# A gated MLP's down-projection by one level of Strassen instead of plain tiles, with sums of weights and gated values kept in DRAM

## The chip, the cores and the metric

One core of one Trainium2 chip. The time is device microseconds of one execution; the kernel before takes 2624.11 us (median of 3 runs, 2624.06 to 2625.13). The engines are named as in the profile: PE (TensorE, matmuls), PEld (its weight loads), DVE (VectorE), ACT (ScalarE), POOL (GpSimd), SP (SyncE, which issues every DMA).

## The reference, cut to what matters

Two layers of an encoder over 1024 tokens of 1024 channels, float32. Each layer has a token mixer (layer 0 attention, layer 1 pooling), a cross-attention into 256 memory tokens, and a gated MLP; residual adds around each. The part that changes is the end of the MLP:

```python
def conv_gated_ffn(h, w_up, conv_w, conv_b, w_down):
    u = h @ w_up                                   # 1024 x 1024 by 1024 x 5632
    up = jnp.pad(u, ((0, 0), (1, 1), (0, 0)))
    u = up[:, :-2] * conv_w[0] + up[:, 1:-1] * conv_w[1] + up[:, 2:] * conv_w[2] + conv_b
    gate, val = u[..., :D_FF], u[..., D_FF:]
    return (jax.nn.silu(gate) * val) @ w_down      # 1024 x 2816 by 2816 x 1024
```

## The kernel before

**Precision.** Every large product is made in three matmuls (`mm3`, L583 to L588): each operand is split into a high part (ACT, L498) and the rest (DVE, L501), and high x high, high x low and low x high are added up in PSUM. An operand of 512 columns thus costs one ACT and one DVE instruction of 512 before PE can use it.

**Buffers.** `scr` is a pool of six tiles of 128 x 1024 that serves every load and scratch value. `R` holds 20 slots, or 40 "halves" of 128 x 1024, for split operands. `X0` to `X7` are the residual rows, 128 tokens each. PSUM has two tiles of two banks (`pA`) and four of one bank (`pB`) in this part.

**Order of the MLP**, the same in both layers:

1. *Output projection of the cross-attention*, `Seven.begin`, 16 steps written out by hand. Step (n, t) makes columns n of token tile t with 24 matmuls, and DVE adds them to `X[t]` (L1087). Where n is 1 the row is complete: SP stores it to `Xd` in DRAM (L231), ACT, POOL and DVE normalise it in place (L567, L559, L236), and PE transposes it one step later (`turn`, L241; steps 3, 4, 6, 8, 10, 12 and 15). The transposed tiles go on as operands of a Strassen form of seven products (`Seven`). `extras` hangs loads and sums of the first weight blocks on some steps.
2. *Up-projection*: 22 blocks f of 128 gate and 128 value channels, each in seven products of 12 matmuls (`Seven.product`). For each block SP loads two tiles of weights (L292), DVE makes four sums of them (L311), ACT and DVE split seven operands, and read the products from PSUM (L355, L357). Then come the convolution (L1110, L1115, L1120), SiLU (L1127) and the gate (L1131); the gated block, 128 channels x 1024 tokens, is stored to `G` in DRAM (L1134). The eight `X` tiles serve as weight buffers here, four to a block.
3. *Down-projection*: six rounds of up to four blocks. A round loads its blocks of `G` and of `w_down` into `scr` (L1154), splits them into halves, and for each token tile t and column half n adds 3 matmuls per block in one bank, which DVE adds to `X[t]` (L1239). The rows come back from `Xd` (L1224). Rounds are prefetched while the round before runs; the last one, blocks 20 and 21, is interleaved with what follows: in layer 0 the pooling mixer (its weights are loaded by `late`, called one round earlier; its first matmul is L1315), in layer 1 the final norm.

**Who sets the order.** In step 2 and the first loads of step 3 a planner (`Plan`) is given every instruction with a price, dependencies, buffer needs and a due time; it lists them greedily and the program is emitted in that order, so each engine's queue is fixed by it. A load is priced as 0.40 us of SP and 4.2 us until it has landed, whatever else is in flight. PE's own order is fixed by hand (`order`). In steps 1 and 3 the order is that of the code.

Of the kernel before, what the change touches and what calls it, by code (L numbers as in the profile page):

```python
# [16 lines left out]
P = 128  # L17
# [24 lines left out]
N_SLOTS = 20  # L42

# [73 lines left out]
class Plan:  # L117
# [4 lines left out]
    KINDS = {"product": ("PE", 2.72, 2.92), "turn": ("PE", 0.87, 1.07), "add": ("DVE", 0.60, 0.72),  # L122
             "add2": ("DVE", 1.14, 1.25), "tap": ("DVE", 1.20, 1.31), "copy": ("ACT", 0.51, 0.65),
             "copy2": ("ACT", 0.96, 1.10), "centre": ("ACT", 1.15, 1.28), "silu": ("ACT", 0.96, 1.10),
             "load": ("SP", 0.40, 4.20), "store": ("SP", 0.40, 4.20)}
# [8 lines left out]
    def add(self, kind, emit, reads=(), writes=(), take=(), uses=(), gives=None, late=None):  # L134


        engine, busy, lag = self.KINDS[kind]
# [22 lines left out]
    def run(self):  # L160
# [6 lines left out]
        left = {e: [op for op in self.ops if op["engine"] == e] for e in self.free}  # L167
        uses = {k: len(ops) for k, ops in self.users.items()}
        takers = [op for op in self.ops if op["take"]]

        def begin(op):

            if any(o["end"] is None for o in op["after"]):
                return None
            t = max([self.free[op["engine"]], op["begin"]] + [o["end"] for o in op["after"]])
            need = {}
            for pool, _ in op["take"]:
                need[pool] = need.get(pool, 0) + 1
            for pool, n in need.items():
                first = sum(p == pool for o in takers if o["end"] is None and o["due"] < op["due"] for p, _ in o["take"])  # L180
                if len(self.room[pool]) < n + first:
                    return None
                t = max(t, sorted(self.room[pool])[n - 1])
            return t if op["engine"] == "PE" else max(t, op["due"] - self.AHEAD)

        while any(left.values()):
            best = None
            for e, ops in left.items():
                found = [(t, op) for op in (ops[:1] if e == "PE" else ops) if (t := begin(op)) is not None]
# [27 lines left out]
class Seven:  # L217
# [76 lines left out]
    def first_load(self, f, n):  # L294

        self.raws[f] = [self.kn.scr() for _ in range(n)]
        self.place[f] = [f"raw{f}{j}" for j in range(4)]
        for j in range(min(n, 2)):
            self.load(f, j)

    AT = {"A11": (0, 0), "A12": (0, 1), "A21": (1, 0), "A22": (1, 1), "S1": (2, 0), "S2": (2, 1), "S3": (3, 0), "S4": (3, 1)}
    SUMS = {"S1": ("A21", "A22", OP.add), "S2": ("S1", "A11", OP.subtract), "S4": ("A12", "S2", OP.subtract),
            "S3": ("A11", "A21", OP.subtract)}
# [61 lines left out]
    def begin(self, gemm, add, free, between):  # L365
# [5 lines left out]
        extras = {1: between, 2: lambda: self.first_load(0, 4), 6: lambda: self.first_load(1, 1),  # L371
                  7: lambda: [self.sum(0, n) for n in self.SUMS],
                  14: lambda: (split(0, "A12", "A11"), late("T2", 1), late("T2", 3)),
                  15: lambda: late("T3", 1)}
        for i, (n, t) in enumerate(steps):
# [7 lines left out]
            if n:  # L383
                self.rows(t)
            if u is not None:
# [6 lines left out]
    def plan_rest(self, plan):  # L392
# [4 lines left out]
        def keep(name, t, src, *keys, uses=()):  # L397
            parts = lambda: self.parts(name, t)
            shaped = lambda: src().rearrange("p (a b) -> p a b", a=4)
            plan.add("copy", lambda: self.kn.high(list(parts())[0], shaped()), keys, [("H", name, t)], uses=uses)  # L400
            plan.add("add", lambda: self.kn.low(*parts(), shaped()), [*keys, ("H", name, t)], [("H", name, t)], uses=uses)

        def sub(out, p, q, reads, writes, uses=(), late=None):
            plan.add("add", lambda: self.sub(nc.vector, out(), p(), q()), reads, writes, uses=uses, late=late)
# [7 lines left out]
        plan.add("turn", lambda: self.turn(t), [X(t, 0), X(t, 1)], banks, [("B", k) for k in banks])  # L412
        plan.add("copy", lambda: nc.scalar.copy(y[:, lo], self.ps[t][0]), banks[:1], [X(t, 0)], uses=banks[:1])
# [15 lines left out]
    def plan_load(self, plan, f, *js):  # L429
        for j in js:  # L430
            plan.add("load", partial(self.load, f, j), (), [(self.place[f][j], h) for h in range(2)], uses=[self.place[f][j]])
# [5 lines left out]
    def plan_left(self, plan, f, sums, names):  # L437
        for n in sums:
            spots = [self.spot(f, m) for m in (*self.SUMS[n][:2], n)]
            plan.add("add", partial(self.sum, f, n), spots[:2], spots[2:], uses={s[0] for s in spots})  # L440
        for n in names:
            at, op = self.spot(f, n), ("op", f, n)
            plan.add("copy", partial(self.high, f, n), [at], [op], [("half", op)], at[:1])
            plan.add("add", partial(self.low, f, n), [at, op], [op], uses=[at[0], op])

    def plan_product(self, plan, f, n, last):
# [7 lines left out]
        plan.add("product", emit, [op] + [("H", right, t) for t in (1, 3, 5, 7)], [(bank, f)],  # L454
# [4 lines left out]
        plan.add(how, partial(self.read, f, n, how),  # L459
# [4 lines left out]
class Kernel:  # L464
# [634 lines left out]
    def ffn_main(self, i, U, X, Xd, late, begin):  # L1099
        nc, R = self.nc, self.R  # L1100
        wd = self.a["ffn_w_down"][i]
        G = self.tc.dram_tile([FF, S], F32, name=f"G{i}")
        C = {}

        def taps(name, j):

            def centre(f):
                u, c = U.bank[f][name], self.scr()
# [16 lines left out]

        def silu(f):
# [6 lines left out]
        def store(f):  # L1133
            nc.sync.dma_start(out=G[f * P:(f + 1) * P, :], in_=C.pop(("v", f)))  # L1134

        def plan_conv(plan, name, f):
            u, c = (name, f), ("conv", name, f)
            ins = [(u, 0), (u, 1)]
            centre, left, right = taps[name]
            plan.add("centre", partial(centre, f), ins, [c], [("scr", c)], [u])  # L1140
            plan.add("tap", partial(left, f), [*ins, c], [c], uses=[u, c])
            plan.add("tap", partial(right, f), [*ins, c], [c], uses=[u, c])

        def plan_gated(plan, f, late):
            g, v = ("conv", "g", f), ("conv", "v", f)
            plan.add("add2", partial(gated, f), [g, v], [v], uses=[g, v])
            plan.add("store", partial(store, f), [v], uses=[v], late=late)

        rounds = [list(range(f, min(f + 4, NF))) for f in range(0, NF, 4)]
        hl, raw = {}, {}  # L1150

        def fetch(kind, f):
            raw[kind, f] = self.scr()
            nc.sync.dma_start(out=raw[kind, f], in_=(G if kind == "g" else wd)[f * P:(f + 1) * P, :])  # L1154

        def high(kind, f):
            hs = hl[kind, f] = [R.get_half(), R.get_half()]
            self.high(R.hv(hs[0]), raw[kind, f])

        def low(kind, f):  # L1160
            self.low(*(R.hv(h) for h in hl[kind, f]), raw.pop((kind, f)))

        def operand(kind, f):

            fetch(kind, f)
            high(kind, f)
            low(kind, f)

        def plan_operand(plan, kind, f, late):
            o, parts = ("raw", kind, f), [("part", kind, f, j) for j in range(2)]  # L1170
            plan.add("load", partial(fetch, kind, f), (), [o], [("scr", o)])
            plan.add("copy2", partial(high, kind, f), [o], parts, [("half", None)] * 2, [o])
            plan.add("add2", partial(low, kind, f), [o, *parts], parts, uses=[o], late=late)

        def up():
            begin()
            names = ("A12", "A11", "S1", "S2", "S4", "S3", "A22")
            U.H["T4"] = [R.get(), R.get()]
            plan = Plan({"DVE": 6.5, "ACT": 4.9}, {"scr": 2, "A": 2, "B": 4, "half": len(R.freed)})
            for f, js in ((0, (1, 2, 3)), (1, (0,))):  # L1180
                for j in js:
                    plan.hold("scr", U.place[f][j])
            for name in names[:2]:
                plan.hold("half", ("op", 0, name))
            places = {1: (1, 3, 5), 0: (7, 0, 2, 4), 2: (6, 1, 3, 5)}
# [8 lines left out]
            U.plan_left(plan, 0, (), names[2:])  # L1194
            done = set()
            for item in order:
                if item is None:
                    U.plan_rest(plan)
                    U.plan_load(plan, 1, 1)
                    U.plan_left(plan, 1, U.SUMS, names)  # L1200
# [252 lines left out]
```

## Time and profile before

| what | us |
|---|---|
| median of the runs shown | 2624.11 |
| the profiled execution | 2624.52 |
| its span, first to last instruction | 2622.6 |
| output projection with `begin`, layer 0 | 847 to 946 |
| up-projection, layer 0 | 946 to 1363 |
| down-projection without its last two blocks, layer 0, from the count of its matmuls | 1363 to 1581 |
| the same three in layer 1 | 1858 to 1956, 1956 to 2373, 2373 to 2592 |
| mean granted clock of PE | 0.995 |

The profile is of one execution. Times count from the first instruction. In lists of instructions the columns are start, duration, engine, source line, operation, and the shapes of what is written and read; the bracket gives the engine's idle time just before and what ended it. In tables by stretch they are the stretch, its length, busy time and count of PE, PEld, DVE, ACT and POOL, the clock, the share of the 16 DMA engines that was busy, and GB/s.

### The profile page before, as it was taken

The page shows a single profiled execution, that of the slowest core. Times are in us where ns is not written, and L with a number is a line of the kernel's source. Part 1 is how long each engine was busy: PE and PEld are TensorE (multiplying, and loading weights), DVE is VectorE, ACT ScalarE, POOL GpSimd, SP SyncE. Part 2 cuts the span into 40 slices and gives each one's busy share as a digit, 9 for nine tenths or more (in the row PEclk, how much of TensorE's full clock was granted, in tenths as well). Part 3 has the DMA queues.
Part 4 walks back from the last instruction along what each step waited for, and adds up shares of the span by engine and source line. Part 5 has one row for each costly group of instructions (what it writes and reads, how often), then busy time and mean ns, then how long its engine had stood idle before and what let it go on. Part 6 is the DMA issues. An engine that isn't in the chain of part 4 may idle for free. (4 is left out here: it accounts for less than half of the span.)

```text
span 2622.6 us, 35895 instructions
## 1 busy us (share of the span) xinstructions
PE 2573.9 (98%) x13817; PEld 2203.1 (84%) x13817; DVE 1732.5 (66%) x2479; ACT 1222.9 (47%) x2048; POOL 376.2 (14%) x521
## 2 busy tenths in 40 slices
PE   8989999999999999999999999999999999999998
PEld 7988888888898888888888888889888888888886
DVE  6778999964346379777775435534569777777334
ACT  4448888852245255555552104425446555454111
POOL 3664445520011000000000001102000000000001
PEclk9999999999999999999999999999999999999999
DMA  4200000031223123323254203321313232327201
GB/s 154 85 6 1 1 1 1 1 137 49 88 65 106 49 70 93 95 73 97 73 185 185 96 25 89 106 65 50 106 49 105 78 92 73 97 97 272 90 24 64
DMA packets 167552, 209.20 MB, mean 80 GB/s; under 512 B 6741, under 2 KB 134077, under 8 KB 167381
## 3 DMA queue, kind: packets, MB, share of 16 engines
q1 hardware_dynamic: 167381, 206.91, 24.4%
q8 instruction: 108, 1.77, 0.3%
q14 instruction: 63, 0.52, 0.1%
HBM read 166.42 MB, written 35.65 MB: 77 GB/s over the span
## 5 line engine op out<-in xcount | busy, mean ns | idle before, releaser
L586 PE MATMUL pB<-R,R 128*128 128x512 f32 (+1 forms) x2864 | 1071.2, 375 | 3.8 <-ACT R L506 1.9
L587 PE MATMUL pB<-R,R 128*128 128x512 f32 (+1 forms) x2848 | 1061.3, 373 | 1.7 <-DVE R L507 1.4
L588 PE MATMUL pB<-R,R 128*128 128x512 f32 (+1 forms) x2784 | 1035.7, 372 | 0.0
L586 PEld LDWEIGHTS pB<-R,R 128*128 128x128 f32 x2864 | 538.7, 188 | 101.5 <-ACT R L506 3.1
L587 PEld LDWEIGHTS pB<-R,R 128*128 128x128 f32 x2848 | 536.4, 188 | 96.0 <-DVE R L507 4.0
L588 PEld LDWEIGHTS pB<-R,R 128*128 128x128 f32 x2784 | 524.1, 188 | 92.0 <-DVE R L507 0.2
L1239 DVE TENSOR_TENSOR X<-pB,X 128x512 f32<-128x512 f32 x192 | 131.2, 688 | 225.0 <-PE pB L588 224.9
L501 DVE TENSOR_TENSOR R<-X,R 128x512 fp32r<-128x512 f32 x310 | 209.9, 686 | 91.2 <-ACT R L498 91.2
L559 POOL TENSOR_SCALAR ms<-ss 128x1 f32<-128x1 f32 (+2 forms) x102 | 26.6, 260 | 1697.4 <-ACT scr L567 781.2
L498 ACT ACTIVATE R<-X 128x512 fp32r<-128x512 f32 x310 | 193.3, 631 | 89.9 <-PE pB L587 71.8
L498 ACT ACTIVATE R<-scr 128x1024 fp32r<-128x1024 f32 (+1 forms) x106 | 100.3, 981 | 246.3 <-PE pB L587 160.7
L580 PE MATMUL pB<-ident,scr 128*128 128x128 f32 x1376 | 182.3, 276 | 10.8 <-DVE scr L572 9.1
L580 PEld LDWEIGHTS pB<-ident,scr 128*128 128x128 f32 x1376 | 157.3, 142 | 37.8 <-POOL scr L672 14.7
L672 POOL TENSOR_SCALAR scr<-scr,inv 128x1024 f32<-128x1024 f32 x128 | 144.0, 1125 | 167.1 <-DVE inv L671 162.2
L507 DVE TENSOR_TENSOR PT<-pB,PT 128x512 fp32r<-128x512 f32 x256 | 163.9, 680 | 3.2 <-ACT PT L506 2.3
L669 ACT ACTIVATE scr<-pA,nm 128x1024 f32<-128x1024 f32 x128 | 142.9, 1116 | 44.7 <-DVE nm L666 41.5
L355 ACT COPY scr<-pB 128x512 f32<-128x512 f32 x132 | 77.4, 586 | 183.5 <-PE pB L588 182.2
L666 DVE TENSOR_REDUCE nm<-pA 128x1 f32<-128x1024 f32 x128 | 156.1, 1220 | 0.9 <-PE pA L662 0.4
L506 ACT ACTIVATE R<-pB 128x512 fp32r<-128x512 f32 (+1 forms) x182 | 94.4, 551 | 127.4 <-PE pB L588 80.4
L507 DVE TENSOR_TENSOR R<-pB,R 128x512 fp32r<-128x512 f32 (+1 forms) x182 | 108.6, 627 | 65.1 <-ACT R L506 64.8
L662 PE MATMUL pA<-R,R 128*128 128x512 f32 x512 | 146.6, 408 | 0.0
L506 ACT ACTIVATE PT<-pB 128x512 fp32r<-128x512 f32 x256 | 138.7, 596 | 13.1 <-PE pB L580 10.9
(127 smaller groups left out, 3495.9 us busy)
## 6 DMA issues: line engine op xcount, KB each, us to landing
X<-in_ffn_w_up SPq DMA_DIRECT2D x82, 512.0 KB
G<-scr SPq DMA_DIRECT2D x44, 512.0 KB
scr<-in_ffn_w_down SPq DMA_DIRECT2D x44, 512.0 KB
scr<-G SPq DMA_DIRECT2D x44, 512.0 KB
scr<-in_xattn_w_kv SPq DMA_DIRECT2D x32, 512.0 KB
scr<-in_attn_w_qkv SPq DMA_DIRECT2D x20, 512.0 KB
scr<-in_xattn_w_q SPq DMA_DIRECT2D x16, 512.0 KB
scr<-in_xattn_w_o SPq DMA_DIRECT2D x16, 512.0 KB
```

What stands on the lines that cost most here:

```text
L498: self.nc.scalar.activation(hi, src, AF.Copy)
L501: self.nc.vector.tensor_tensor(out=lo, in0=src, in1=hi.bitcast(F32), op=OP.subtract)
L506: nc.scalar.activation(hi, src, AF.Copy)
L507: nc.vector.tensor_tensor(out=lo, in0=src, in1=hi.bitcast(F32), op=OP.subtract)
L580: self.nc.tensor.transpose(p[:, k, :], src[:, b * P:(b + 1) * P], self.ident)
L586: mm(out, ah, bh, start=start, stop=False)
L587: mm(out, ah, bl, start=False, stop=False)
L588: mm(out, al, bh, start=False, stop=stop)
L662: nc.tensor.matmul(s[:, kh * 512:(kh + 1) * 512], q, R.v(K[part][kh], 4)[:, kv], start=part == 0, stop=part == 1)
L666: nc.vector.tensor_reduce(nm, s, axis=AX.X, op=OP.max, negate=True)
L669: nc.scalar.activation(pr, s, AF.Exp, bias=nm, accum_out=rs)
L672: nc.gpsimd.tensor_scalar(pr, pr, ri, 1.0, op0=OP.mult, op1=OP.mult)
```

## The change

The 20 first channel blocks are taken in ten pairs. A pair's values are a matrix of 1024 tokens x 256 channels, its weights one of 256 x 1024; both are cut in two each way, and the pair's part of the result is made in seven products of half the size instead of eight (the same form that the up-projection uses, with the values on the left). The products go in three rounds of 3, 4 and 3 pairs. Blocks 20 and 21 stay as they were, as the last part.

- *Weights*: four differences of each pair's weights are made on DVE during the output projection and stored in DRAM (`ahead`), to be loaded again in the rounds with the four plain quarters that are needed (`plan_W`).
- *Values*: an even block's gated values now stay in `X4`; when the odd block is done, DVE makes four sums, two into `X6` and two in place (`plan_sums`), and SP stores seven pieces of 512 columns to DRAM (`G7`), 256 KB each, instead of two blocks. A round loads them again piece by piece (`plan_G`).
- *Products*: for a round, half of the tokens (g), a product n and a token tile pair (j) there are 3 matmuls per pair into one bank; each of the seven products is read by DVE into `X` (`plan_down`). All of it is given to the planner with the up-projection.
- *Up-projection*: a block has three weight buffers instead of four (S3 and S4 overwrite sources), since `X4` and `X6` are taken; its first loads come at steps 11 and 12 of `begin` instead of 2 and 6, three of block 0's sums at step 13 instead of four at 7.
- *Planner*: an instruction's price is a constant and a part per column; it gives 0.60 us for a DVE instruction of 512 and 2.72 for 12 matmuls, as the fixed prices did.
- `late` (pool weights, layer 0) is called after the plan, just before the last part.

```diff
+NQ = NF // 2 - 1
+ROUNDS = ((0, 1, 2), (3, 4, 5, 6), (7, 8, 9))
...
-    AT = {"A11": (0, 0), "A12": (0, 1), "A21": (1, 0), "A22": (1, 1), "S1": (2, 0), "S2": (2, 1), "S3": (3, 0), "S4": (3, 1)}
+    AT = {"A11": (0, 0), "A12": (0, 1), "A21": (1, 0), "A22": (1, 1), "S1": (2, 0), "S2": (2, 1), "S3": (1, 0), "S4": (2, 1)}
...
-        extras = {1: between, 2: lambda: self.first_load(0, 4), 6: lambda: self.first_load(1, 1),
-                  7: lambda: [self.sum(0, n) for n in self.SUMS],
+        extras = {1: between, 11: lambda: self.first_load(0, 3), 12: lambda: self.first_load(1, 1),
+                  13: lambda: [self.sum(0, n) for n in ("S1", "S2", "S3")],
...
             if n:
                 self.rows(t)
+            ahead(i)
             if u is not None:
                 self.take1(u)
...
-        def store(f):
-            nc.sync.dma_start(out=G[f * P:(f + 1) * P, :], in_=C.pop(("v", f)))
...
+        def plan_sums(plan, q, v, late):
...
+            add(S1, of(one, 1), of(other, 1), OP.add, [o, v], [("X6", 0)], [v])
+            add(S2, S1, of(one, 0), OP.subtract, [("X6", 0), e], [("X6", 1)])
+            add(of(one, 1), of(one, 0), of(one, 1), OP.subtract, [e, o], [o])
+            add(of(one, 0), of(other, 0), S2, OP.subtract, [v, ("X6", 1)], [e], [v])
...
+                plan.add("load", 1, lambda n=n, src=src: keep(n, src(), q), [k], [("G", q, n)], uses=[k], late=late + 2.0)
...
+        def plan_G(plan, r, qs, g, n):
...
+            plan.add("load", 1, fetch, [("G", q, n) for q in qs], [raw], [("scr", raw)])
+            plan.add("copy", w, high, [raw], parts, [("half", k) for k in parts], [raw])
+            plan.add("add", w, low, [raw, *parts], parts, uses=[raw, *parts])
...
+        def ahead(i):
+
+            if i < NQ:
+                raws[i] = [self.scr() for _ in range(2)]
+                for j in range(2):
+                    nc.sync.dma_start(out=raws[i][j], in_=wd[(2 * i + j) * P:(2 * i + j + 1) * P, :])
+            if 0 < i <= NQ:
+                (b11, b12), (b21, b22) = ((r[:, :512], r[:, 512:]) for r in raws.pop(i - 1))
+                for n, (out, p, q) in {"T1": (b11, b12, b11), "T3": (b12, b22, b12), "T2": (b22, b22, b11),
+                                       "T4": (b21, b21, b22)}.items():
+                    nc.vector.tensor_tensor(out=out, in0=p, in1=q, op=OP.subtract)
+                    nc.sync.dma_start(out=WT[i - 1][int(n[1]) - 1], in_=out)
+
+        WAT = (("B21", "B22"), ("B11",), ("T1", "T2"), ("T3", "T4"))
+
+        def plan_W(plan, q, late):
...
+            for j, names in enumerate(WAT):
+                raw = ("wraw", q, j)
+                plan.add("load", 1, partial(fetch, j), (), [raw], [("scr", raw)])
+                for h, n in enumerate(names):
+                    k = ("w", q, n)
+                    plan.add("copy", 512, partial(high, n, j, h), [raw], [k], [("half", k)], [raw])
+                    plan.add("add", 512, partial(low, n, j, h), [raw, k], [k], uses=[raw, k], late=late)
...
+        def plan_down(plan, r, qs, g, j, n):
...
+                for k, q in enumerate(qs):
+                    wh, wl = U.halves(WD[q, right])
+                    self.mm3(banks[b], hi[:, k], lo[:, k], wh, wl, fresh and k == 0, k == len(qs) - 1, not fresh)
...
+            def read():
+                x = X[t][:, h * 512:(h + 1) * 512]
+                nc.vector.tensor_tensor(out=x, in0=banks[b], in1=x, op=OP.add)
+            plan.add("product", 3 * len(qs), emit, parts + ws, [b], [("A" if bank == "x" else "B", b)] if fresh else (),
+                     parts + ws + ([] if fresh else [b]))
+            plan.add("add", 512, read, [b, ("row", t, h)], [("row", t, h)], uses=[b], late=1.5)
+
+        def plan_phase(plan, homes):
...
+            for r, qs in enumerate(ROUNDS):
+                for k, q in enumerate(qs):
+                    plan_W(plan, q, -3.0 * (len(qs) - 1 - k) if k < len(qs) - 1 else None)
+                for g in range(2):
+                    for n in (2, 1, 5, 6, 3, 7, 4):
+                        plan_G(plan, r, qs, g, U.PRODUCTS[n][0])
+                    for n in (2, 1, 5, 6, 3, 7, 4):
+                        for j in range(2):
+                            plan_down(plan, r, qs, g, j, n)
+                            yield
...
-            places = {1: (1, 3, 5), 0: (7, 0, 2, 4), 2: (6, 1, 3, 5)}
+            places = {1: (1, 3), 0: (5, 7, 0), 2: (1, 3, 2)}
+            fixed.update({0: X[4], 1: X[6]})
...
+            phase = plan_phase(plan, places[0] + places[2] + (4, 6))
             for item in order:
+                if item == (4, NF - 1):
+                    next(phase)
...
         with self.tc.manual_schedule():
-            up()
-
-        def down(t, fs):
+            main()
+        late()
+
+        def down(t):
+            fs = range(2 * NQ, NF)
...
-        for r, fs in enumerate(rounds[:-1]):
-            nxt = [(kind, f) for f in rounds[r + 1] for kind in ("g", "d")]
-            if r == len(rounds) - 2:
-                late()
-            for t in range(NT):
-                if nxt:
-                    operand(*nxt.pop(0))
-                down(t, fs)
-            free_round(fs)
-        return lambda t: down(t, rounds[-1]), lambda: free_round(rounds[-1])
+        return down, lambda: R.put_half(*(h for hs in hl.values() for h in hs))
```

More of the change, by code (lines that the diff above doesn't have):

```diff
@@ L117 @@
 class Plan:
[L122 to L125, printed above, removed]
+    KINDS = {"product": ("PE", 0.0, 0.2267, 0.20), "turn": ("PE", 0.0, 0.109, 0.20), "add": ("DVE", 0.067, 0.00104, 0.12),
+             "tap": ("DVE", 0.127, 0.00104, 0.12), "copy": ("ACT", 0.07, 0.00087, 0.135),
+             "centre": ("ACT", 0.26, 0.00087, 0.13), "load": ("SP", 0.0, 0.40, 3.80)}
     AHEAD = 30.0
@@ L1156, in high @@
[L1156 to L1167, printed above, removed]
+            plan.add("centre", 1024, partial(centre, f), ins, c, [] if held(name, f) else [("scr", c[0])], [u])
+            plan.add("tap", 1024, partial(left, f), [*ins, *c], c, uses=[u, *c])
@@ L1199, in up @@
                     U.plan_load(plan, 1, 1)
[L1200 removed]
+                    U.plan_left(plan, 1, *every)
                     continue
```

210 lines of the change are left out of this document (144 added, 66 removed).

## The prediction

> **What bounds the kernel.** I read the page first: busy shares, then the chain, then the costliest groups.
>
> ```profile
> PE 2573.9 (98%) x13817; PEld 2203.1 (84%) x13817; DVE 1732.5 (66%) x2479; ACT 1222.9 (47%) x2048; POOL 376.2 (14%) x521
> ...
> L586 PE MATMUL pB<-R,R 128*128 128x512 f32 (+1 forms) x2864 | 1071.2, 375 | 3.8 <-ACT R L506 1.9
> L1239 DVE TENSOR_TENSOR X<-pB,X 128x512 f32<-128x512 f32 x192 | 131.2, 688 | 225.0 <-PE pB L588 224.9
> ```
>
> PE is busy 98% of the span, and the adds of the down-projection (L1239) idle 225 us, nearly all of it for PE. The 375 ns are a pipelined length; the price of a matmul is the distance between two starts. PE's timeline inside a run gives it:
>
> ```profile
> 866.30 0.39 PE L587 MATMUL pB<-R,R 128*128 128x512 f32 x1
> 866.53 0.39 PE L588 MATMUL pB<-R,R 128*128 128x512 f32 x1
> 866.76 0.39 PE L586 MATMUL pB<-R,R 128*128 128x512 f32 x1
> 866.99 0.39 PE L587 MATMUL pB<-R,R 128*128 128x512 f32 x1
> 867.21 0.39 PE L588 MATMUL pB<-R,R 128*128 128x512 f32 x1
> ```
>
> Five starts in 0.91 us: 0.227 us each. Then the stages of layer 0 (layer 1 agrees within 1 us), as windows of busy time with DMA share and GB/s at the end: the steps of the output projection that get new work; the start and the body of the up-projection; its end with the start of the down-projection; a peak inside that; and, as the last line, a stretch of narrow transfers elsewhere.
>
> ```profile
> 858.00:922.00 64.00, 63.69 (x301) 52.71 (x301) 26.50 (x35) 16.87 (x31) 5.73 (x13) 1.00 0.16 58
> 946.00:1000.00 54.00, 53.83 (x241) 44.12 (x240) 52.68 (x78) 36.66 (x60) 0.00 (x0) 1.00 0.28 88
> 1000.00:1320.00 320.00, 320.00 (x1413) 264.77 (x1412) 253.35 (x326) 164.84 (x239) 0.00 (x0) 1.00 0.30 83
> 1352.00:1398.00 46.00, 46.00 (x204) 37.83 (x203) 34.81 (x37) 20.45 (x21) 0.00 (x0) 1.00 0.89 328
> 1372.00:1390.00 18.00, 18.00 (x81) 14.91 (x80) 12.84 (x15) 7.88 (x8) 0.00 (x0) 1.00 0.98 376
> 1752.80:1765.90 13.10, 13.10 (x109) 12.98 (x109) 9.18 (x12) 6.62 (x10) 0.00 (x0) 1.00 0.76 242
> ```
>
> PE is full in every one, the clock is 1.00, and DVE is at 79% in the body of the up-projection but 98% in its first 54 us. DMA is light until 1352; there it holds 328 GB/s over 46 us, 376 at its peak.
>
> **The term that goes.** Before, a layer's down-projection has 22 channel blocks x 8 token tiles x 2 column halves x 3 = 1056 matmuls. After: 10 pairs x 7 products x 4 token tiles (2 g x 2 j) x 3 = 840, and 2 blocks left over x 8 x 2 x 3 = 96: 936. That is 120 fewer a layer, 240 in all; at 0.227 us, **-54.5 us**. Nothing else is on PE's list. What follows asks whether PE can stay full.
>
> **The output projection (new: `ahead`).** In its steps 0 to 10 a layer now loads 20 weight blocks of 512 KB, makes 40 differences on DVE and stores 40 pieces of 256 KB: 10.5 + 10.5 MB. Five of those steps also store a row tile (L231, 0.52 MB each): 23.6 MB. Without turns a step is 24 x 0.227 = 5.45 us, a turn adds 0.87: 11 steps with 5 turns are 64 us. The first two loads go out before step 0, since SP runs ahead (it issued the table's loads at 839.6 while PE reached step 0 at 847). How fast can this move? 58/0.16 = 362 and 328/0.89 = 369 GB/s at full share; sustained 328. I take 350: 23.6 MB need 67 us, against 64. So DMA is about full here, and the question is who waits for it. The timeline of DVE and of PE's weight loads tells:
>
> ```profile
> 893.54 0.69 DVE L1087 TENSOR_TENSOR X<-pB,X 128x512 f32<-128x512 f32 x1 [0.35 <-PE pB L588]
> 897.91 1.28 DVE L236 SCALAR_TENSOR_TENSOR X<-X,rs,scr 128x1024 f32<-128x1024 f32 x1 [3.68 <-DMA Xd<-X]
> ...
> 899.25 0.86 PEld L241 LDWEIGHTS pB<-ident,X 128*128 128x128 f32 x8 [0.74 <-DVE X L236]
> ```
>
> The norm (L236) overwrites the row that L231 is storing, so it waits for the store; the turn of that tile waits for the norm. The store of 864.28 freed its norm 2.75 us later, this one (issued 894.26) 3.65 later, and the 0.9 us became 0.74 us of PE idle: **the row store has no slack**. Four of the seven turns start within 0.1 us of their norm. On DVE the four differences (0.60 us each; six splits of that size, L501, take 3.69) stand between the add and the norm; 2.4 us fit into the 2.75 that it waits already, if their loads have landed.
>
> I carried the queue through the steps by hand: 0.8 us from issue to the first packet and 0.45 after the last (what the 2.75 leave beside 1.5 us of moving), 1.5 us per 512 KB, a transfer after all issued before it, a load held until its buffer's store has landed. The row store of step 2 finds the engines free. That of step 3 (869.7) stands behind the load and stores issued from 864.7 on and moves from 872.6 instead of 870.5; its norm ends at 875.9, PE is there at 875.3: 0.6 us. Steps 5, 7 and 9 lose 1.7, 1.8 and 1.7 likewise. About 5.8 a layer: **+11.5 us**. At 376 GB/s the traffic takes 63 us, and nothing need be lost; at 328, 72, some 8 plus 2 for the queue: 0 to 20 for both. The first loads of block 0 move from step 2 to step 11, behind this traffic, and three of its sums from step 7 to 13: two steps, 11 us, for a load, and DVE idled 1.3 and 2.3 us around its adds of 929.4 and 934.9, room for 1.8. Nothing; without that room, 1.8 us in the stretch that follows.
>
> The Trainium skill, "DMA: Bandwidth & Descriptors", section "Bandwidth", puts the HBM side's limit for a core at about 358 GB/s. By it these bytes take 66 us, an estimate from that page, 2 over PE's 64; the trace's 376 in a short peak is above it, its 328 over 46 us below.
>
> **The up-projection.** Per pair, DVE gets four more 512-wide sums (2.4 us in 38); one sum of block 0 moves into the first 54 us, in which DVE has 1.3 us free and PE already waited for it once (layer 1: 0.31 us at 1999.14, released by L357). Of the sums only that 0.6 us has a due time in there: +1 a layer, **+2** (0 to 6). In the body DVE goes from 79% to 85%; three buffers for a block instead of four hold the same two loads, S3 and S4 overwriting sources that are already read or split; products still find 12 halves of operands ahead. The planner's prices per instruction stay what they were. Stores rise from 512 KB to 7 x 256 KB per two blocks, small beside 83 GB/s. **+1** (0 to 6).
>
> **The down-projection.** PE's Strassen part is 840 x 0.227 = 191 us a layer. DVE in it: 84 reads x 0.69 = 58; 70 weight splits x 0.60 = 42; 28 splits of 768 and 14 of 1024 at about 0.9 and 1.2 = 42: 142 us, 74%. ACT has half of that. Uneven it is at the first half of a round: in a round of three pairs a group of two products is 18 x 0.227 = 4.1 us of PE and 3 x 0.60 + 0.9 + 2 x 0.69 = 4.1 of DVE. Without work done ahead DVE would be the bound there. What covers it is the end of the up-projection, which has no next block to prepare: between 1330 and 1365 DVE was busy 24.9 of 35 us, of which eight operands at 1.2 were 9.7. Free for operands are thus about 20 us, against the 19 that the first half-round needs. DMA: three pairs' weights 5.5 MB, values 2.8, rows back 4.2 = 12.5, in a stretch that moved 15.2 MB (46 us at 328) with PE full. The second halves (16 of 29 us on DVE) prepare the next round. The tightest read is between products 7 and 4 on one bank, one product (2.0 us) apart: a split in the way 1.2 + read 0.69 + 0.2 is about 2.1, tenths each. I take +2.5 a layer, **+5**; if nothing were prepared the first group would cost a load (4.8 us in the chain of waits), a copy and 2.7 of DVE, so 0 to 10 a layer.
>
> **Pool weights (layer 0).** They were fetched a round (43 us) before the last part; now they stand behind the whole plan on every queue, 22 us before its end. On DVE that is 8 scalings (0.4) and 2 splits (1.2), 5.6 us, ahead of the first read of the last part; PE has four banks, two parts of 2.7 us, to run on. Loss about 2, and as much in the existing 3.9 us wait of the mixer (L1315 for ACT): **+4** (0 to 10).
>
> **Sum.** 2624.5 (the profiled execution: span 2622.6 and 1.9 around it) - 54.5 + 11.5 + 2 + 1 + 5 + 4 = 2593.5. That execution is 0.4 above the median of 2624.1, so **2593**, 1.2% less; its own range is 2583 to 2608.
>
> **Rivals.**
> 1. *All is hidden*: DMA runs at its 376, DVE keeps ahead. For it: the start of the down-projection moved 15.2 MB without a PE gap. Against: no slack at the turns. 2570 to 2583.
> 2. *Row stores land late for another reason than the queue*: the store at 894.26 had the engines to itself and still took 0.9 us more. Were all ten once to twice that late beside loads and stores from HBM, 9 to 18 us come on top: 2603 to 2612, and with a transition that is not prepared up to 2629. The Trainium skill, same page, section "Latency and other measured facts", speaks for it: HBM's access latency is 0.2 us on average and 2 us at high load; no run so far shows that.
> 3. *Slower*: the mixed traffic of `ahead` is paced by its buffers (five, two taken a step, each held from load through difference to landed store) instead of the engines. A stretch whose loads wait for buffers, 1752.8 to 1765.9, moved 242 GB/s at a share of 0.76. At 242 the 23.6 MB take 98 us, 34 over, all of it on the turns: 2593.5 - 11.5 + 2 x 34 = 2650. It decides from 277 GB/s on: 54.5 - 12 = 42.5, 21 a layer, 85 us. Against it: a load has a step and more from issue to use.
> That the matmuls do not fall is excluded by the count.
>
> **Chances.** Forecast 0.45, rival 1 0.25, rival 2 0.17, slower 0.13. A difference of 0.2% (5 us) is about what a measurement can tell from none. Faster: 0.45 + 0.25 + 0.11 of rival 2 = 0.81; same 0.06 (rival 2's end); slower 0.13. The range, 2571 to 2625, holds the first two and nearly all of the third, 0.85.
>
> **What would show it.** 936 matmuls a layer in the down-projection at 0.227; DMA near full and `Xd` waits of L236 over 3.5 us in steps 3 to 9, with PE gaps only before L241; no PE gaps within rounds; a gap near L1315 larger than 3.9. PE gaps in the body of the up-projection, or at every round's start, would mean that DVE or the halves were the matter and my sum wrong; gaps of 3 us or more at the turns mean rival 3.

## The result, and the profile after

The changed kernel takes **2611.3 us** (median of 5 runs, 2608.4 to 2612.9) against 2624.5 (2624.1 to 2625.5) for the kernel before: a ratio of 0.9948 (95% interval 0.9933 to 0.9962), or 13.2 us less. The forecast was 2593, 31 us less. The direction was right and the time lies in the whole range of 2571 to 2625, but outside the forecast's own 2583 to 2608: less than half of the expected gain arrived. The profiled execution took 2610.45 us, its span 2608.7, which is 13.9 less than the span before.

From the page of the changed kernel, the engines and the same two groups as shown of before (L601 was L586, and L1296 takes the place of L1239):

```profile
PE 2536.9 (97%) x13577; PEld 2166.9 (83%) x13577; DVE 1911.3 (73%) x2791; ACT 1298.5 (50%) x2192; POOL 378.1 (14%) x521
...
L601 PE MATMUL pB<-R,R 128*128 128x512 f32 (+1 forms) x2728 | 1023.1, 376 | 4.5 <-ACT R L521 1.9
...
L1296 DVE TENSOR_TENSOR X<-pB,X 128x512 f32<-128x512 f32 x144 | 99.2, 690 | 87.8 <-PE pB L603 85.3
```

The 240 matmuls are gone (13817 to 13577), and DVE has 179 us more. The count alone is worth 54.5 us, so some 40 came back somewhere. The windows of the changed kernel say where; the columns are those of the windows before:

```profile
860.00:926.00 66.00, 61.46 (x275) 50.02 (x274) 44.92 (x64) 15.12 (x28) 5.23 (x10) 0.95 0.91 319
941.00:1000.00 59.00, 58.90 (x266) 48.31 (x266) 50.08 (x74) 35.83 (x59) 1.48 (x4) 1.00 0.21 63
1000.00:1320.00 320.00, 320.00 (x1414) 265.05 (x1413) 276.80 (x368) 164.01 (x239) 0.00 (x0) 1.00 0.38 111
1352.00:1398.00 46.00, 43.38 (x186) 34.22 (x185) 36.58 (x48) 25.14 (x37) 0.00 (x0) 1.00 0.84 290
```

The up-projection (second and third line) is as full as it was: 1414 matmuls in 320 us, where before had 1413, and DVE at 86.5%. The output projection (first line) has 275 matmuls in 66 us, at a clock of 0.95, with DMA at a share of 0.91 and 319 GB/s. The same stretch of the kernel before has 314:

```profile
860.00:926.00 66.00, 65.69 (x314) 54.51 (x313) 28.47 (x37) 18.09 (x33) 6.02 (x14) 1.00 0.16 56
```

The start of the down-projection (last line of the windows after) has 186 in 46 us instead of 204.

DVE's timeline of the changed kernel at a turn, the place that the prediction had named; the store of the row was issued at 870.5:

```profile
869.79 0.69 DVE L1102 TENSOR_TENSOR X<-pB,X 128x512 f32<-128x512 f32 x1 [0.36 <-PE pB L603]
870.87 0.69 DVE L1244 TENSOR_TENSOR scr<-scr 128x512 f32<-128x512 f32 x1 [0.39 <-DMA scr<-in_ffn_w_down]
872.45 2.14 DVE L1244 TENSOR_TENSOR scr<-scr 128x512 f32<-128x512 f32 x3 [0.88 <-DMA scr<-in_ffn_w_down]
877.00 1.28 DVE L246 SCALAR_TENSOR_TENSOR X<-X,rs,scr 128x1024 f32<-128x1024 f32 x1 [2.41 <-DMA Xd<-X]
```

The norm (L246) starts 6.5 us after the issue (3.2 for the same row before), and what it waits for is `Xd`, the row store. The differences (L1244) are done 2.41 us earlier. PE's timeline of the same kernel just after it:

```profile
878.34 1.26 PE L251 MATMUL pB<-ident,X 128*128 128x128 f32 x8 [2.23 <-DVE X L246]
...
880.34 0.63 PE L603 MATMUL pB<-R,R 128*128 128x512 f32 x1
880.77 0.63 PE L601 MATMUL pB<-R,R 128*128 128x512 f32 x1
881.20 0.63 PE L602 MATMUL pB<-R,R 128*128 128x512 f32 x1
```

The turn waits 2.23 us for the norm, as predicted in kind. Then comes something that the prediction did not have: the matmuls start 0.43 us apart, not 0.227. A window of the same kernel over these starts has the granted clock in its third column from the right:

```profile
879.60:883.20 3.60, 3.60 (x9) 2.84 (x10) 3.50 (x6) 1.60 (x4) 0.00 (x0) 0.53 0.92 339
```

The trace records the clock at 0.50 from 879.82 on for 3.41 us. Three turns a layer stall for about 2 us or more: 2.4, 2.5 and 4.0 us in layer 0, 1.9, 2.6 and 3.3 in layer 1. With five of the six comes a record of half clock: 3.41 us soon after the stall, or 6.83 at the longest one of each layer, where it begins 1.2 and 0.9 us before the stall ends; only the 1.9 us left the clock alone. Before, the output projection has no such record in either layer.

**A ledger.** For each pair of matmul starts I take the distance less 0.227 us. Distances over 0.30 us are counted as idle, and the surplus of those made at half clock is kept apart. Both layers together, after less before:

| stage | idle | half clock | cost | predicted |
|---|---|---|---|---|
| output projection | 19.7 - 2.1 | 9.0 - 0 | 26.6 | 11.5 (0 to 20) |
| up-projection, start and body | 1.3 - 1.7 | 0 | -0.4 | 3 (0 to 12) |
| down-projection with its start | 9.6 - 0.4 | 0 | 9.2 | 5 (0 to 20) |
| mixer of layer 0 (pool weights) | 7.2 - 4.2 | 0.8 - 0.1 | 3.7 | 4 (0 to 10) |

The sum is 39.1, and 54.5 - 39.1 = 15.4, within 1.5 us of the 13.9 by which the spans differ.

A second measure needs no threshold. In each layer, up to the down-projection, PE runs the same matmuls in the same order in both kernels, so the start of each can be compared with its start before. By that the output projection costs 14.7 us in layer 0 and 13.1 in layer 1, 27.8 together: 16.6 of stalls, 8.0 of matmuls of 512 columns at half clock, and 3.1 of the turns' transposes, which the ledger leaves out. The ledger's first row and its two parts are thus good to about 1 us. Below, the cost of the output projection is given by this second measure, from one trace of each kernel; *spread* and the three kernels built on it, whose code is the same there, differ by up to 2.7 us.

### The profile page after: what moved, and what is told of

The parts are those of the page before. It is cut to its first block, busy times and chain, and to the rows that moved or that the text cites. A ratio compares the mean times of both kernels' runs of the same rounds, so it can differ in the third digit from the quotient of the medians.

```text
span 2608.7 us, 36701 instructions
## 1 busy us (share of the span) xinstructions
PE 2536.9 (97%) x13577; PEld 2166.9 (83%) x13577; DVE 1911.3 (73%) x2791; ACT 1298.5 (50%) x2192; POOL 378.1 (14%) x521
## 3 DMA queue, kind: packets, MB, share of 16 engines
q8 instruction: 107, 1.75, 0.3%
## 4 chain that ended last, share of the span: by engine, by line
PE 76%; DVE 11%; DMA 4%; ACT 4%; issue 3%; POOL 2%; SPq 0%; DVEq 0%; ACTq 0%; POOLq 0%
PE pB L603 20%; PE pB L602 20%; PE pB L601 20%; PE pB L595 3%; PE pA L603 3%; PE pA L601 3%; PE pA L602 3%; DVE nm L681 2%; PE pA L677 2%; DMA scr<-in_ffn_w_down 1%; DMA Xd<-X 1%; PE pB L908 1%; DVE PT L522 1%; POOL qn L753 1%; PE pB L909 1%
## 5 line engine op out<-in xcount | busy, mean ns | idle before, releaser
L601 PE MATMUL pB<-R,R 128*128 128x512 f32 (+1 forms) x2728 | 1023.1, 376 | 4.5 <-ACT R L521 1.9
L603 PE MATMUL pB<-R,R 128*128 128x512 f32 (+1 forms) x2748 | 1025.0, 373 | 1.7 <-DVE R L516 1.7
L602 PE MATMUL pB<-R,R 128*128 128x512 f32 (+1 forms) x2728 | 1018.0, 373 | 1.7 <-DVE R L522 1.4
L601 PEld LDWEIGHTS pB<-R,R 128*128 128x128 f32 x2728 | 515.9, 189 | 98.6 <-ACT R L521 3.1
L603 PEld LDWEIGHTS pB<-R,R 128*128 128x128 f32 x2748 | 519.5, 189 | 93.7 <-DVE R L516 2.5
L602 PEld LDWEIGHTS pB<-R,R 128*128 128x128 f32 x2728 | 516.2, 189 | 92.6 <-DVE R L522 4.0
L513 ACT ACTIVATE R<-scr 128x512 fp32r<-128x512 f32 (+2 forms) x250 | 176.0, 737 | 211.2 <-PE pB L602 68.8
L516 DVE TENSOR_TENSOR R<-scr,R 128x512 fp32r<-128x512 f32 (+2 forms) x250 | 197.9, 821 | 19.4 <-ACT R L513 19.4
L1296 DVE TENSOR_TENSOR X<-pB,X 128x512 f32<-128x512 f32 x144 | 99.2, 690 | 87.8 <-PE pB L603 85.3
L601 PE MATMUL pA<-R,R 128*128 128x512 f32 (+1 forms) x448 | 156.3, 349 | 6.0 <-ACT R L521 2.1
L603 PE MATMUL pA<-R,R 128*128 128x512 f32 (+1 forms) x448 | 155.3, 347 | 1.1 <-DVE R L522 0.8
```

The lines of the kernel that those rows point to most:

```text
L513: self.nc.scalar.activation(hi, src, AF.Copy)
L516: self.nc.vector.tensor_tensor(out=lo, in0=src, in1=hi.bitcast(F32), op=OP.subtract)
L601: mm(out, ah, bh, start=start, stop=False)
L602: mm(out, ah, bl, start=False, stop=False)
L603: mm(out, al, bh, start=False, stop=stop)
L1296: nc.vector.tensor_tensor(out=x, in0=banks[b], in1=x, op=OP.add)
```

## The experiments

Each ratio is to the kernel before on the same chip. The first four ran together on one chip, then the next four, then the last three. "After" means the changed kernel.

**Is it the order in the queue?** In the first, the row store has a queue of its own; in the second, the loads and stores of a step come behind its splits; the third does both.

```diff
-        self.nc.sync.dma_start(out=self.Xd[t * P:(t + 1) * P, :], in_=self.X[t])
+        self.nc.scalar.dma_start(out=self.Xd[t * P:(t + 1) * P, :], in_=self.X[t])
```

> The changed kernel, but the row stores of the output projection are issued by ACT instead of SP, so that they have a queue of their own. Theory A (the row store stands behind the weight traffic in one queue, 5.6 to 6.4 us until its norm starts instead of 2.75): the store shares the engines instead of waiting, about 4 us; turns lose at most 1.3 us each, no gap is long enough for the clock to fall to half, and of the 26.6 us that the output projection lost some 18 come back: about 2593. Theory B (on DVE the four differences, with their waits for loads, stand before the norm): nothing changes, 2608 to 2613.

Measured: 2613.9 us (2611.3 to 2616.6), 0.9957 [0.9942, 0.9972]; no gain over after. Its issue of that store, in the timeline of ACT of this kernel:

```profile
872.07 0.33 ACTq L241 DMA_DIRECT2D Xd<-X  x1
```

The norm of the same row, in DVE's timeline of this kernel:

```profile
871.96 2.86 DVE L1244 TENSOR_TENSOR scr<-scr 128x512 f32<-128x512 f32 x4
879.01 1.28 DVE L246 SCALAR_TENSOR_TENSOR X<-X,rs,scr 128x1024 f32<-128x1024 f32 x1 [4.20 <-DMA Xd<-X]
```

Issued on a queue with nothing else in it, the store still takes 6.9 us until its norm can start; of the five others beside this traffic in layer 0, four take 4.4 to 5.7 and one 3.2. Its first packet starts 2.8 us after the issue and its last ends after 6.3; the store of 894.26 before, with the engines to itself, has 0.8 and 3.1. The stretch from 860 to 926 moves 323 GB/s at 0.90, as in after. The store's place in SP's queue is thus not what delays it: it shares the 16 engines with the rest. The time alone would not show this. The stalls of layer 0 are more even (five of 1.3 to 2.5 us), and the output projection costs 24.9 us instead of 27.8, all of the difference in layer 0; but the down-projection with the mixer costs 18.6 instead of 13.2, with 3.41 us of half clock at its start in each layer, where after has none. Why it does was not tried. The Trainium skill, "DMA: Bandwidth & Descriptors", section "Issuing engines are not separate DMA queues", says that DMAs started by several engines end on the same 16 and interleave; these 6.9 us agree.

```diff
-            ahead(i)
...
+            ahead(i)
```

> The changed kernel, but each step's weight traffic and differences come at the end of the step, behind the norm and the splits. Theory B (differences and their waits hold up the norm on DVE): the stalls at the turns go, about 2588 to 2594. Theory A (the queue): the row store of a step still stands behind the transfers of the step before, 2603 to 2611.

Measured: 2631.0 us (2628.8 to 2634.3), 1.0022 [1.0012, 1.0032], slightly slower than before, which neither theory had. The output projections cost 44.9 us, and stalls reach 7.8 us. The stretch moves less, not more; the window of this kernel from 860 on:

```profile
860.00:936.00 76.00, 68.43 (x303) 54.91 (x301) 48.43 (x69) 16.97 (x31) 5.11 (x12) 0.96 0.80 284
```

SP's waits in this kernel, from 860 to 945 (total us, times, longest):

```profile
SPq L1245 <- DVE scr L1244: 49.0, 39, 9.6
```

SP's waits in after in the same stretch:

```profile
SPq L1245 <- DVE scr L1244: 15.6, 15, 9.6
SPq L241 <- DVE X L1102: 13.7, 5, 3.9
SPq L1239 <- DMA Wt<-scr: 12.0, 5, 3.1
```

The differences now come behind the splits on DVE, so their stores go out later (49 us of waits instead of 15.6; the last at 934.0 instead of 925.0), and SP, whose list is in a fixed order, comes to the next loads later (the third pair's after 860 at 883.1 instead of 876.6). The 16 engines get less to do, and the same bytes take longer. Traffic paced by something other than the engines is what the prediction's third rival had; but it had the buffers in mind, and the loads' own wait for one (L1239) falls from 12.0 to 2.3 us in all. What holds them back here is their place behind late stores.

> Both edits at once: row stores issued by ACT, weight work at the end of the step. Theory A alone: as with the first edit alone, about 2593. Theory B alone: as with the second alone. If each holds back what the other frees, only this one comes near the floor of 2585 (2611.3 less the 26.6 lost in the output projection): 2586 to 2592.

Measured: 2639.5 us (2637.4 to 2642.5), 1.0055 [1.0040, 1.0070]; 270 GB/s at 0.75 from 860 to 936, and 54.1 us for the output projections. Neither theory had this either. The own queue makes the second edit worse instead of mending it.

**What does the stretch cost, and which part of it?** Three kernels leave work out: the whole of `ahead`, the four differences alone, and the stores alone. Where nothing is stored, the rounds load as many plain weights. The first:

```diff
-            begin(ahead)
+            begin(lambda i: None)
```

> The changed kernel without any weight work in the output projection: the differences are left out of the computation, and the rounds load plain weights of the same size in their place. By the ledger of the trace (26.6 us lost there, 17.6 idle and 9.0 at half clock) 2611.3 - 26.6 = 2585. If the loss were in the up- or down-projection instead, it would stay at 2600 or more.

Measured: 2587.7 us (2582.7 to 2588.0), 0.9853 [0.9838, 0.9868]. By the medians the stretch costs 23.6 us, three less than in the ledger. In the trace the output projection falls from 27.8 us to 0.7, and the down-projection with the mixer costs 16.7 instead of 13.2, which is the difference.

```diff
-                    nc.vector.tensor_tensor(out=out, in0=p, in1=q, op=OP.subtract)
```

> The changed kernel without the differences of the weights: the same loads, buffers and stores, but the stored quarters are the plain weights, so that DVE does 24 us a layer less in the output projection. Theory D (bytes): no change, 2607 to 2613. If DVE's work and its waits in front of the norm are the cause: 2590 to 2600.

Measured: 2609.1 us (2603.1 to 2610.6), 0.9936 [0.9921, 0.9951], as after. Its window:

```profile
860.00:926.00 66.00, 59.85 (x269) 48.95 (x268) 21.35 (x27) 15.90 (x29) 5.00 (x11) 0.95 0.89 308
```

DVE has half the work (21.35 us instead of 44.92), and the stalls and the clock stay: the output projections cost 26.2 us.

```diff
-                    nc.sync.dma_start(out=WT[i - 1][int(n[1]) - 1], in_=out)
```

> The changed kernel with the loads and differences of the weights, but without their stores: the rounds load plain weights of the same size in their place, so the differences are left out of the result. 13.1 MB instead of 23.6 in 64 us, 205 GB/s. Theory D: the stalls at the turns nearly go, 2588 to 2593. If the differences in front of the norm cost by themselves: 2600 or more.

Measured: 2588.4 us (2586.0 to 2589.5), 0.9860 [0.9845, 0.9875]. Its window:

```profile
860.00:926.00 66.00, 64.24 (x307) 53.07 (x306) 49.56 (x69) 17.46 (x32) 7.40 (x13) 1.00 0.57 200
```

With the DVE work kept and nearly half of the traffic gone, the stalls are nearly gone and the clock is 1.00: the output projections cost 3.5 us, against 27.8. So it is the traffic, not DVE's work. Whether it is the bytes, the number of transfers or that these are stores, this run cannot tell, since all of them go together.

**Can the same bytes be had for less?** The first two pairs are loaded at step 0, the loads end at step 10 instead of 9 and the stores at 12 instead of 10, so that most steps get less. The first loads of the up-projection move to steps 12 and 13.

```diff
+        STEPS = {0: "S0", 1: "L2", 2: "S1", 3: "L3 S2", 4: "L4", 5: "S3 L5", 6: "S4", 7: "L6 S5", 8: "L7", 9: "S6 L8 S7",
+                 10: "L9", 11: "S8", 12: "S9"}
```

> The changed kernel with the same weight work spread over the steps: two pairs are loaded ahead of step 0, then about one half-unit a step (a pair's load, or its differences and stores), two where the next step stores no row, the last at step 12; block 0's first loads at steps 12 and 13. Theory D (the stretch is bound by the bytes that the DMA engines move: 23.6 MB at 320 to 340 GB/s are 69 to 74 us against PE's 64): the same bytes over some 85 us leave the engines free when a row store comes; no gap over 2 us, no half clock, 26.6 lost become some 8: 2593. If a row store is late beside any transfer at all (rival 2 of the prediction, 0.9 us at 14 turns): about 2598. If bytes and their timing are not the cause: 2608 to 2613.

Measured: **2592.5 us** (2590.5 to 2594.0), 0.9876 [0.9862, 0.9891]: 19 us of the 23.6 come back, with every byte and every difference still made. The windows of this kernel, the old stretch and the new one:

```profile
860.00:926.00 66.00, 63.39 (x300) 52.32 (x298) 43.34 (x60) 16.88 (x31) 7.71 (x13) 1.00 0.81 288
852.00:941.00 89.00, 84.89 (x398) 69.76 (x398) 61.53 (x87) 21.13 (x39) 9.01 (x14) 1.00 0.77 270
```

At 288 GB/s and 0.81 the row stores come back in time more often, and the output projections cost 8.1 us instead of 27.8. The stretch is longer by two steps in which DMA had been light. The longest stall that is left, 2.29 us in each layer, has another cause: at step 9 eight differences stand before the norm on DVE (from 907.42 to 913.01 in layer 0), and the norm follows them without a wait for its store.

**Is the pool weights' term what it was said to be?** The kernel before, with `late()` called after its rounds and nothing else changed:

```diff
-            if r == len(rounds) - 2:
-                late()
...
+        late()
```

> The kernel before with one edit: the pool weights of layer 0 are fetched after the fifth round instead of before it, as the changed kernel has it. My prediction priced this at +4 us (0 to 10): 2628. The two traces show the wait before the mixer's first matmul grow from 4.1 to 6.2 us and the half-clock time behind it from 3.4 to 6.8: +2 to +4. If that growth came from another part of the change: no difference.

Measured: 2628.6 us (2626.4 to 2629.8), 1.0013 [1.0003, 1.0023], or 3.8 us more than before (0.8 to 6.0 by the interval). The mixer's wait in this kernel, in PE's timeline:

```profile
1595.95 3.75 PE L1314 MATMUL pA<-scr 128*128 128x112 f32 x16 [6.12 <-ACT scr L1307]
```

The same in PE's timeline of after:

```profile
1587.38 3.76 PE L1466 MATMUL pA<-scr 128*128 128x112 f32 x16 [6.06 <-ACT scr L1459]
```

The two agree within 0.1 us (3.89 before). The term of 4 was right in size, and the longer wait comes from the place of `late`.

**What ends the start of the down-projection?** In after, PE loses 4.1 us between 1366 and 1392, in five gaps of 0.3 to 1.1 us and some smaller ones, mostly waiting for operands. SP's waits in after from 1340 to 1395:

```profile
SPq L1256 <- DVE scr L1138: 8.1, 1, 8.1
SPq L1256 <- DVE R L516: 7.4, 4, 2.4
SPq L1216 <- DVE scr L1156: 4.4, 1, 4.4
```

L1256 and L1216 load weights and values of the rounds into `scr`, and wait for a buffer. The longest hold is by the convolution of the last blocks (L1138, L1156), the others by the splits. Is it that, or the due times of the weights, by which the planner lets the first round's loads go late? The three kernels stand on *spread*, and change only the planner's wishes:

```diff
-                    plan_W(plan, q, -3.0 * (len(qs) - 1 - k) if k < len(qs) - 1 else None)
+                    plan_W(plan, q, None)
```

> The kernel with the spread weight work (2592.5), and the weights of every round due when their product needs them, instead of all seven operands of the first pairs some 3 to 9 us before the round. Theory E: at the start of the down-projection (3.9 and 3.7 us idle there) the six buffers hold weights of late products while the first product waits for its values and its third pair's weights; in order of need 5 to 7 us of the 8 come back: about 2586. Rival F: the buffers are simply too few while the last blocks' convolution holds four of them, whatever the order: 2590 to 2594. Rival G: later rounds, prepared less early, begin to wait: above 2594.

Measured: 2593.4 us (2592.0 to 2594.6), 0.9878 [0.9862, 0.9895], as *spread*, and as theory F has it. The stall moves and stays. PE's timeline of this kernel has it here:

```profile
1376.27 0.50 PE L601 MATMUL pB<-R,R 128*128 128x512 f32 x1 [2.22 <-DVE R L515]
```

And its waits of SP from 1340 to 1395:

```profile
SPq L1215 <- DVE R L515: 12.0, 9, 3.7
SPq L1263 <- DMA scr<-Gs: 4.8, 1, 4.8
SPq L1263 <- DVE scr L1137: 4.3, 1, 4.3
SPq L1265 <- DVE scr L1137: 3.8, 1, 3.8
```

SP still waits for buffers: most for those that the splits hold (L515), then for those of the convolution (L1137 here). The next drops the due times in the first round alone:

```diff
-                    plan_W(plan, q, -3.0 * (len(qs) - 1 - k) if k < len(qs) - 1 else None)
+                    plan_W(plan, q, -3.0 * (len(qs) - 1 - k) if r and k < len(qs) - 1 else None)
```

> As the run before, but only the first round's weights are due in order of need; the others keep their early due times. Theory E: 2586, as before. Rival G: this one gains, the run before does not. Rival F: 2590 to 2594.

Measured: 2598.3 us (2596.1 to 2598.7), 0.9894 [0.9879, 0.9908], some 5 us worse, which none of the theories had: the start loses 11.6 us over both layers and 2.5 at half clock, where *spread* loses 10.3 and 1.5, and a stall of 1.7 us turns up later in each layer (1430 and 2429), which *spread* does not have. Due times do not lift it. The last lets the planner prepare work 45 us ahead instead of 30:

```diff
-    AHEAD = 30.0
+    AHEAD = 45.0
```

> The kernel with the spread weight work (2592.5), but the planner may start an instruction 45 us before its due time instead of 30. If the start of the down-projection waits because its loads are allowed too late: 4 to 6 us less, 2587. By theories E and F nothing: 2590 to 2595, since the queue already waits for buffers there.

Measured: **2589.0 us** (2588.4 to 2590.7), 0.9861 [0.9846, 0.9876], the fastest of all that make the whole computation. That is between the two expectations. The start loses 2.7 and 3.6 us and 1.4 at half clock, against 5.2, 5.1 and 1.5 in *spread*; a new stall of 1.7 us in the up-projection of layer 1 (2074) takes some of it back. Its interval overlaps that of *spread*, and the two ran on the chip at different times, so that the 3.5 us between them come from `AHEAD` alone is likely, not shown.

## Why the prediction was right or wrong, point by point

- **The term that goes** was right: 240 matmuls, and 0.227 us each wherever PE ran at full clock.
- **The output projection** is the step that failed. Its chain was right: the norm waits for the row store, the turn waits for the norm, and there is next to no slack. DMA was indeed near full, and leaving out the stores (*no_wt_store*) makes the stalls go, while leaving out DVE's work (*no_diffs*) does not. Its size was wrong twice. First, the rate: I took 350 GB/s, and the stretch moved 319 at a share of 0.91. That is 350 for a share of 1, so the engines were as fast as I took them to be, but not always busy. The 23.6 MB then take 74 us, not 67, against the 64 that PE needs. The hand-carried queue gave stalls of 0.6 to 1.8 us; they were 2 to 4. With idle alone the term would have been 17.6 instead of 11.5, inside its bounds. Second, I priced a stall at its length. Five of the six stalls of about 2 us or more brought 3.41 or 6.83 us of half clock, which cost 9.0 us in all, and that put the term at 26.6 (27.8 by the second measure) and outside its bounds. The nearest rows could have warned: the kernel before has its own 3.41 us record from 1591.95 on, at the end of the mixer's wait of 3.89 us, and I did not look at the clock there. One reading was a little off: in the trace before, two turns in layer 0 and one in layer 1 start within 0.1 us of their norm, not four of seven; most start 0.4 to 0.5 us after it.
- The carrying by hand also took the order of issue as the order of landing. *row_on_act* shows that this is not what decides: alone in its queue, the store took as long (6.9 us; 6.5 in after).
- **The up-projection** cost nothing measurable (-0.4 against 3). DVE at 86.5% (predicted 85) still left PE full: 1414 matmuls in 320 us. The 0.6 us of due work a layer that I had charged to its first stretch were absorbed.
- **The down-projection** cost 9.2 instead of 5, inside its 0 to 20. I had argued from DVE's free time (20 us against 19). At its start in after, PE waited for operands whose loads waited for one of the six buffers of `scr`, up to 8.1 us for a tile that the convolution of the last blocks holds. That these waits set the loss is read from the trace and not shown: no run had more buffers. Moving the due times (*due_all*, *due_first*) does not help, and *ahead_45*, which lets loads go earlier, seems to take some 4 us back, which speaks for loads let go too late as a part of it.
- **The pool weights** cost 3.7 by the ledger and 3.8 by an experiment of their own, against 4. In part this is luck: the mixer's wait grew by 2.2 us as forecast, but the other 2, before the last part's first read, did not come (from 1512 to 1581.5, just ahead of that wait, PE is busy for 69.1 of 69.5 us). Other small gaps and half clock stand in their place.
- **The rivals.** All hidden (2570 to 2583) did not come, and even with `ahead` left out the time is 2587.7. The second (2603 to 2629) gave the right time, and half of its reason: row stores do land late beside this traffic, three a layer only 4.3 to 6.5 us after their issue instead of 2.7 to 3.7, but it did not have the clock. The third did not come in after, which moved 319 GB/s. Its lower rates came in *ahead_last* and *both*, at 284 and 270 and through late stores instead of scarce buffers, and these were slower than before. The bound that I gave for it, 277 GB/s, left out the clock: 284 was already slower. The sign that I gave for it, gaps of 3 us or more at the turns, was wrong: after has two of them (4.0 and 3.3) at 319 GB/s.
- The forecast 2593 is what *spread* takes, with 2592.5; but that is no confirmation, since it is another order of issue: its output projections cost 8.1 us where I had 11.5, and its down-projection with the mixer 16.2 where I had 9.

## What to carry to other kernels

Where a transfer is on the path to PE and other transfers fill the engines, spread those over the steps in which DMA is light before anything else: the same bytes at 288 instead of 319 GB/s gave back 19 of 23.6 us, and a queue of its own shortened nothing. Price a stall of PE with the clock that may follow it, which here added 9.0 us to 17.6 us of idle. When work is moved later on DVE, look at which stores wait for it and which loads stand behind these in the queue, since that can set the rate.

## What the runs showed of the hardware that was not expected

The clock falls to half after short gaps: by the ledger's measure, stalls of 2.4 to 2.6 us in after were followed by 3.41 us at 0.50, those of 3.3 and 4.0 us came with 6.83, and one of 1.9 us with nothing; at half clock matmuls of 512 columns start 0.43 us apart instead of 0.227. The Trainium skill, "TensorE: Matmul & The Clock Gate", Part 1, states the two states, a free-running window of 3413 ns and 426.7 ns for such a matmul when cold, and the records and starts here agree with each. It puts the return to half clock at one idle window or more, about 3.4 us; here 2.4 us of idle was enough, so for this the measurement decides. By that 3.4 us the stall of 4.0 us alone could have cost anything beyond itself.

The length alone does not decide. *Spread* has a stall of 2.29 us in each layer: the one that ends at 1909.40 was followed by 3.41 us at 0.50, the one that ends at 914.34 by nothing, and in *both* two of 2.6 and 2.7 us were followed by nothing. In each of the thirteen traces the records of half clock after the first 210 us begin whole multiples of 3.413 us apart, as on a fixed grid. The 2.29 us that were followed lie in one step of that grid; the grid cuts the other 2.29 into 1.75 and 0.54, and the two of *both* into 1.37 and 1.21, 1.36 and 1.30. These cases suggest that the idle time within one step counts, which is not shown: steps with 1.8 to 2.1 us of idle went either way.

Loads and stores mixed moved 319 GB/s at a share of 0.91 here, while the start of the down-projection before the change reached 376 at 0.98 for 18 us. What makes the difference, the share of stores, the rows of 512 columns or the number of transfers in flight, was not tried and stays open.
